# One pass over x about a pivot, single-tile adaLN units and extra adaLN buffers at the start of a layer step

## The chip, the core and the metric

The kernel runs on one core of a Trainium2 chip. The metric is the device time of one execution in microseconds (us). The engines are named as the profile names them: PE is TensorE (PEld its weight load), DVE is VectorE, ACT is ScalarE, POOL is GpSimd, and SP is SyncE, which does no arithmetic here and only issues transfers. "Clock" is the TensorE clock that the chip granted, as a share of full speed.

## The reference, cut to what matters

One layer of a language model, for 256 prompt tokens and 8 samples of 4 tokens, 288 tokens in all, with 2048 features in fp32. What the change touches is the first line of the layer, the modulation and the first normalisation:

```python
mod = silu(c) @ w_ada + b_ada                 # adaLN: 6 x 2048 numbers per sequence (9 sequences)
sh1, sc1, g1, sh2, sc2, g2 = split(mod, 6)
h = layer_norm(x) * (1 + sc1) + sh1           # (x - mean) * rsqrt(var + eps), over the 2048 features
z = h @ w_in                                  # 2048 x 7176
... # two recurrent mixers, w_out, a convolutional feed-forward part (w_up, w_down), two more norms
```

## The kernel before

All activations lie with features on the 128 partitions and tokens along the free axis, so x is 16 tiles (KT) of 128x288. Every weight product is exact to fp32 by halves: a weight block and its input are each split into a high part (`whi`, cast on ACT) and a low part (`wlo`, raw minus high on DVE), and three matmuls are made of each 128x128 block. Weights come in granules of 512 KB (8 blocks, 24 matmuls), one DMA each; `granule()` keeps the raw loads five granules ahead (`load_to`), the high halves three (`high_to`) and the low halves two (`low_to`). The adaLN matrix `w_ada` comes in 512 KB pieces too; an `ada_step` multiplies one of them. Steps are grouped into units: a unit gives the shift and the scale of a few feature tiles of h, and `ADA_K` lists how many tiles the first units give. All of these loads are on SP's queue, in program order, and an issue that finds eight transfers under way waits until the oldest has landed.

`start()` is the stage around the change. It loads c (`ct`), the 16 tiles of x with a DMA each, seven pieces of `w_ada`, then the constants `cs` and `pks` (the bias of adaLN is in the latter). It takes the mean with column sums on PE (`colsum`, `total`: a copy on ACT and a second matmul), subtracts it from each tile (every third tile on POOL, the others on DVE), squares (every fourth on DVE, the others on ACT), sums again, and makes the reciprocal deviation `rx` of it (`rstd_of`). Eight adaLN steps are spread between. Then the product with `w_in` begins in four groups of input tiles (KG = 2, 2, 4, 4): each group runs over 28 output tiles, needs only as many tiles of h as its number says, and adds its partial sums into `z` (`partial`: a copy out of PSUM on ACT for the first group, an addition on DVE for the others). Between the granules come batches of four adaLN steps. When a unit is complete, `ada_finish` transposes it on DVE (`adsb`), adds the bias (`mod`), and queues `hidden(k)` for its tiles: x times `rx`, times the scale, plus the shift, for the prompt and for the samples, and one tick later the split into halves. PSUM has two banks for `mm`, five for `sd`, one for `ad`; a matmul that starts a new sum waits until the bank was read out. DVE, ACT and PE each run in program order.

The lines that the prediction follows, besides the functions below, are these of `low_to` and `high_to`, and the end of the stage in `mixer()`, which loads the rest of `pks` and needs it for a few small DVE operations (`hgrn_lb`) ahead of the next low half:

```python
self.nc.scalar.copy(hi[:, :w], raw[:, :w])                                   # high_to, ACT
self.tt(lo[:, :w], raw[:, :w], hi[:, :w].bitcast(F32), ALU.subtract)         # low_to, DVE
nc.sync.dma_start(self.cs[:, a:], i["cst"][:, a:])                           # mixer
nc.sync.dma_start(self.pks[:, b:], i["pk"][:, b:])
```

Of the kernel before, what the change touches and what calls it, by code (L numbers as in the profile page):

```python
# [10 lines left out]
F32 = mybir.dt.float32  # L11
# [3 lines left out]
ALU = mybir.AluOpType  # L15
PSUM = bass.MemoryType.PSUM

P = 128
D = 2048
KT = 16  # L20
# [3 lines left out]
T = TP + NB * TS  # L24
# [5 lines left out]
EPS = 1e-5  # L30
# [6 lines left out]
NR = 7  # L37
NQ = 5
NA = 7
BATCH = 4  # L40
NS = 4
RATE = 1.3
RA = 2
NPRE = 12
AD0 = 176
# [2 lines left out]
WIDTH = 3  # L48
SPACING = 5
KG = (2, 2, 4, 4, 4)  # L50
ADA_K = (2, 2, 2, 2, 4, 4)
NSPLIT = 28
NUP = 3
LEVELS = (1, 2, 4, 8, 16, 32, 64)
# [71 lines left out]
def _ada_units():  # L126

    u, k = [], 0
    for n in ADA_K:
        u.append([16 * m + k + q for m in range(2) for q in range(n)])  # L130
# [8 lines left out]
class K:  # L139
# [28 lines left out]
    def mm(self, out, lhsT, rhs, start, stop, **kw):  # L168
        self.nc.tensor.matmul(out, lhsT, rhs, start=start, stop=stop, **kw)  # L169
# [112 lines left out]
    def later(self, *fs):  # L282

        def run():
            for f in fs:
                f()
                yield
        self.bg.append(run())
# [7 lines left out]
    def ada_load(self, n):  # L296
        while len(self.ad_raw) < min(n, self.ad_limit):
            s = len(self.ad_raw)
            ahead = 0 <= s - AD0 < NPRE
            if not ahead and s >= (self.ad_n if s < AD0 else max(self.ad_n, AD0 + NPRE)) + NA:  # L300
                break
            if ahead:
                raw = self.pre.tile([P, 1024], F32, tag="apre", name=self.nm("apre"), bufs=NPRE)
            else:
                raw = self.wp.tile([P, 1024], F32, tag="araw", name=self.nm("araw"), bufs=NA)
            self.nc.sync.dma_start(raw, self.i["w_ada"][s])
            self.ad_raw.append(raw)

    def ada_batch(self):

        while self.credit >= BATCH:
            self.credit -= BATCH
            for _ in range(BATCH):
                self.ada_step()

    def ada_step(self):


        s = self.ad_n
        if s >= self.ad_stop:  # L320
            return
        self.ad_n += 1
        self.ada_load(s + NA)
        raw, (u, g) = self.ad_raw[s], STEPS_ADA[s]
        w = 32 * len(UNITS_ADA[u])
        nk = 256 // w
        if g == 0:
            if self.ad_pend is not None and self.ad_pend[0]:
                next(self.ad_pend[1])
            self.ad_ps = self.ps(w, self.ad_tag if u % 2 else "ad")  # L330
        for z in range(nk):
            k = nk * g + z
            for q in range(4):
                c = (4 * z + q) * w
                self.mm(self.ad_ps[32 * q:32 * q + 32], self.csp[:, k, :], raw[:, c:c + w], k == 0, k == KT - 1)
        if k == KT - 1:
            self.ad_pend = [True, None]
            self.ad_pend[1] = self.ada_finish(u, self.ad_ps, self.ad_pend)
            self.bg.append(self.ad_pend[1])
# [69 lines left out]
    def run(self):  # L409
        nc, tc, ctx, i = self.nc, self.tc, self.ctx, self.i  # L410
        self.misc = ctx.enter_context(tc.tile_pool(name="misc", bufs=1))
        self.wp = ctx.enter_context(tc.tile_pool(name="wp", bufs=1))
        self.psum = ctx.enter_context(tc.tile_pool(name="psum", bufs=1, space=PSUM))
        one = self.misc.tile
        self.cs = one([P, NCC], F32, name="cs")
        self.pks = one([P, NPK], F32, name="pks")
        self.mod = one([P, 96, 9], F32, name="mod")
        self.csp = one([P, KT, 32], F32, name="csp")
        self.lm = one([P, len(LEVELS), T // 2], U8, name="lm")
        self.ones = one([P, P], F32, name="ones")  # L420
        nc.gpsimd.memset(self.ones, 1.0)
        self.onesr = one([P, P], F32R, name="onesr")
        nc.gpsimd.tensor_copy(self.onesr, self.ones)
        self.eps = one([P, 1], F32, name="eps")
        nc.gpsimd.memset(self.eps, EPS)
        nc.scalar.preload_act_table_set("natural_log_exp_and_others")
        self.queue_weights()
        self.active, self.bg, self.since, self.credit, self.rate = [], [], 99, 0.0, 0.0
        self.ad_raw, self.ad_n, self.ad_pend, self.h = [], 0, None, []
        self.ad_stop, self.ad_limit, self.ad_tag = AD0 - 4, AD0, "sd"  # L430
        self.start()
        self.mixer()
        self.tail()

    def start(self):

        nc, i = self.nc, self.i
        ct = self.t288()[:, :KT * 9].rearrange("p (k c) -> p k c", c=9)
        nc.sync.dma_start(ct, i["ct"])
        xs = self.xs = [self.t288() for _ in range(KT)]  # L440
        for k in range(KT):
            nc.sync.dma_start(xs[k], i["xt"][:, k, :])
        self.ada_load(NA)
        a, b = CC["cap"][0], PK["b_ada"][1]
        nc.sync.dma_start(self.cs[:, :a], i["cst"][:, :a])
        nc.sync.dma_start(self.pks[:, :b], i["pk"][:, :b])
        nc.gpsimd.memset(self.csp, 0.0)
        e = self.t288()[:, :KT * 9].rearrange("p (k c) -> p k c", c=9)
        self.act(e, ct, AF.Abs)
        self.act(e, e, AF.Exp, scale=-1.0)  # L450
        self.act(e, e, AF.Ln, bias=1.0)
        self.stt(e, ct, 0.0, e, ALU.min, ALU.subtract)
        self.act(e, e, AF.Exp)
        self.tt(self.csp[:, :, 0:9], ct, e, ALU.mult)
        sm = self.ps(T)
        for k in range(KT):
            self.colsum(sm, xs[k], k, KT)
        mu = self.t288()
        self.tsc(mu, self.total(sm), 1.0 / (32 * D), None, ALU.mult)
        self.ada_step()  # L460
        self.ada_step()
        sq = self.ps(T)
        for k in range(KT):
            self.tt(xs[k], xs[k], mu, ALU.subtract, eng=nc.gpsimd if k % 3 == 2 else None)
            s = self.t288()
            if k % 4 == 3:
                self.tt(s, xs[k], xs[k], ALU.mult)
            else:
                self.act(s, xs[k], AF.Square)
            self.colsum(sq, s, k, KT)  # L470
            if k % 4 == 1:
                self.ada_step()
        var = self.t288()
        self.tsc(var, self.total(sq), 1.0 / (32 * D), EPS, ALU.mult, ALU.add)
        self.rx = self.rstd_of(var)
        self.h = []
        self.z = [self.t288() for _ in range(NSPLIT)]
        self.load_to(2)
        for _ in range(2):
            self.tick()  # L480
            self.ada_step()
        k0, done = 0, 0
        for g, ks in enumerate(KG[:-1]):
            while len(self.h) < k0 + ks:
                self.tick()
            nj = GK // ks
            for p in range(NSPLIT // nj):
                hl = self.granule()
                for j in range(nj):
                    ps = self.ps(T, "sd" if j % 2 else "mm")  # L490
                    self.products(ps, hl, j * ks * P, self.h[k0:k0 + ks], True, True)
                    self.tick()
                    self.bg.append(self.partial(self.z[nj * p + j], ps, g == 0))
                self.credit += 2 if done < 14 or done % 3 == 0 else 1
                self.ada_batch()
                done += 1
            k0 += ks
        while len(self.h) < KT:
            self.tick()
# [8 lines left out]
    def hidden(self, k):  # L508
        x = self.xs[k]
        hf = self.t288()  # L510
        self.tt(x, x, self.rx, ALU.mult)
        self.tsc(hf[:, :TP], x[:, :TP], self.mp(1, k), self.mp(0, k), ALU.mult, ALU.add)
        self.tt(self.smp(hf), self.smp(x), self.ms(1, k), ALU.mult)
        self.tt(self.smp(hf), self.smp(hf), self.ms(0, k), ALU.add)
        yield
        self.h.append(self.split(hf))
# [848 lines left out]
    def tail(self):  # L1365
        nc, i, r = self.nc, self.i, self.r
        with self.tc.tile_pool(name="pre", bufs=1) as self.pre:
# [4 lines left out]
            for p in range(KT // 2):  # L1372
# [6 lines left out]
                while self.ad_n < min(AD0, AD0 - 4 + 2 * p):  # L1379
                    self.ada_step()  # L1380
                self.ada_load(AD0 + min(NPRE + NA, 2 * p))
            self.low_to(self.w_used + NL - 1)
# [230 lines left out]
```

## Time and profile before

| | us |
|---|---|
| median of 3 runs | 1605.6 (1604.3 to 1609.29) |
| the profiled execution | 1606.86 |
| its span in the trace | 1605.1 |
| mean granted clock of TensorE in it | 0.985 |
| busy: PE, DVE, ACT, POOL | 1545.0 (96%), 1032.5 (64%), 696.1 (43%), 297.4 (19%) |

The profile is of one execution. A row of its timeline gives the start, the duration or extent of a run of equal instructions, the engine, the line of the code, the operation with its output and inputs, the count, and in brackets how long the engine stood idle before and what released it.

### The profile page before, as it was taken

The numbers are of one execution on the slowest core, as the hardware profiler recorded it, in microseconds if no ns is written. First come the engines' busy times: TensorE is split into PE (matmuls) and PEld (weight loads), VectorE is DVE, ScalarE is ACT, GpSimd is POOL, SyncE is SP. The second block draws the span as 40 slices with busy tenths as digits, with TensorE's granted clock in tenths as the row PEclk, the third lists the DMA queues.
The fourth block names the chain that finished last, engine by engine and source line by source line (L and its number), as shares of the span: only waits on it lengthen the run. The fifth ranks groups of instructions, "written<-read, shape, count | busy, mean of one in ns | idle before, by whom it ended". The sixth has DMA issues, their size and how long they took to land.

```text
span 1605.1 us, 31742 instructions
## 1 busy us (share of the span) xinstructions
PE 1545.0 (96%) x12577; PEld 1449.7 (90%) x12577; DVE 1032.5 (64%) x2068; ACT 696.1 (43%) x1222; POOL 297.4 (19%) x450
## 2 busy tenths in 40 slices
PE   6999989999999989998999999999999999999995
PEld 3999879788898878886999999999999999999994
DVE  4566656888788779778855555455555555555465
ACT  3522325565656555335643433344343333434343
POOL 1000001444353443225311100011110001111012
PEclk9999999999999999998999999999999999999997
DMA  9898855778868778781545455554555555555551
GB/s 337 331 339 325 302 175 159 263 255 302 301 232 294 287 256 312 264 327 64 193 158 170 161 161 171 166 168 162 170 161 159 167 170 170 162 168 158 152 161 60
DMA packets 99268, 340.79 MB, mean 212 GB/s; under 512 B 11432, under 2 KB 18096, under 8 KB 98096
## 3 DMA queue, kind: packets, MB, share of 16 engines
q1 hardware_dynamic: 96624, 328.55, 59.9%
q0 software_dynamic: 2496, 10.22, 1.6%
q8 instruction: 99, 1.62, 0.4%
q14 instruction: 49, 0.40, 0.1%
HBM read 326.51 MB, written 12.21 MB: 211 GB/s over the span
## 4 chain that ended last, share of the span: by engine, by line
PE 83%; DVE 10%; ACT 3%; DMA 3%; issue 1%; SPq 1%; POOL 0%; ACTq 0%; DVEq 0%
PE mm L169 68%; PE sd L169 11%; DVE t L156 4%; PE ad L169 3%; DVE wlo L156 1%; DVE t L159 1%; ACT t L166 1%; DVE t L163 1%; ACT whi L229 1%; DVE c L159 1%; DMA raw<-w_in_b 1%; DMA t<-xt 1%; DMA pks<-pk 1%; DMA raw<-w_out_b 0%; DMA araw<-w_ada 0%
## 5 line engine op out<-in xcount | busy, mean ns | idle before, releaser
L169 PE MATMUL mm<-t,whi 128*128 128x288 f32 (+1 forms) x4624 | 939.2, 298 | 17.0 <-ACT whi L229 9.2
L169 PEld LDWEIGHTS mm<-t,whi 128*128 128x128 f32 (+1 forms) x4624 | 742.9, 189 | 31.3 <-ACT whi L229 12.2
L169 PE MATMUL mm<-t,wlo 128*128 128x288 f32 x2312 | 684.4, 296 | 7.9 <-DVE wlo L156 7.8
L229 ACT CAST whi<-raw 128x1024 fp32r<-128x1024 f32 (+2 forms) x413 | 423.2, 1027 | 472.8 <-PE mm L169 240.2
L156 DVE TENSOR_TENSOR wlo<-raw,whi 128x1024 fp32r<-128x1024 f32 (+2 forms) x413 | 502.7, 1218 | 21.4 <-ACT whi L229 15.9
L169 PEld LDWEIGHTS mm<-t,wlo 128*128 128x128 f32 x2312 | 435.7, 188 | 9.8 <-DVE wlo L156 9.8
L169 PE MATMUL mm<-ff,whi 128*128 128x288 f32 x1376 | 276.1, 296 | 0.0
L169 PEld LDWEIGHTS mm<-ff,whi 128*128 128x128 f32 x1376 | 220.6, 188 | 3.4 <-issue 2.3
L169 PE MATMUL mm<-ff,wlo 128*128 128x288 f32 x688 | 203.1, 295 | 0.0
L166 ACT ACTIVATE t<-t 128x288 f32<-128x288 f32 (+4 forms) x328 | 125.5, 396 | 172.7 <-DVE t L156 111.8
L156 POOL TENSOR_TENSOR t<-t,t 128x288 f32<-128x288 f32 (+3 forms) x159 | 143.1, 909 | 283.9 <-ACT t L166 102.0
L159 DVE SCALAR_TENSOR_TENSOR t<-mm,mod,t 128x256 f32<-128x256 f32 x96 | 46.3, 482 | 149.7 <-PE mm L169 141.6
L169 PEld LDWEIGHTS mm<-ff,wlo 128*128 128x128 f32 x688 | 129.1, 188 | 0.0
L1412 POOL COPY convo<-ext 128x2 f32<-128x2 f32 x43 | 8.0, 186 | 630.4 <-ACT ext L1406 630.4
L156 DVE TENSOR_TENSOR t<-t,t 128x288 f32<-128x288 f32 (+5 forms) x219 | 106.3, 505 | 27.1 <-ACT t L189 20.2
L1407 DVE COPY ext<-mm 128x32 f32<-128x32 f32 x42 | 8.1, 193 | 140.9 <-ACT ext L1406 140.9
L169 PE MATMUL sd<-t,whi 128*128 128x288 f32 x464 | 95.6, 298 | 0.0
L169 PE MATMUL ad<-araw,csp 128*32 128x256 f32 (+1 forms) x1312 | 75.8, 362 | 0.7 <-DMA araw<-w_ada 0.7
L169 PEld LDWEIGHTS sd<-t,whi 128*128 128x128 f32 x464 | 75.8, 192 | 0.0
L156 DVE TENSOR_TENSOR t<-cv,mm 128x256 f32<-128x256 f32 x80 | 20.7, 300 | 79.0 <-PE mm L169 79.0
L169 PE MATMUL sd<-t,wlo 128*128 128x288 f32 x232 | 69.2, 298 | 0.0
L156 DVE TENSOR_TENSOR t<-t,mm 128x288 f32<-128x288 f32 x70 | 31.5, 450 | 56.1 <-PE mm L169 55.8
(233 smaller groups left out, 1151.9 us busy)
## 6 DMA issues: line engine op xcount, KB each, us to landing
araw<-w_ada SPq DMA_DIRECT2D x180, 512.0 KB, 5.4
raw<-w_up_b SPq DMA_DIRECT2D x160, 512.0 KB, 3.6
raw<-w_in_a SPq DMA_DIRECT2D x56, 512.0 KB, 6.8
raw<-w_in_b SPq DMA_DIRECT2D x56, 512.0 KB, 6.5
raw<-w_down SPq DMA_DIRECT2D x48, 512.0 KB, 3.5
raw<-w_down SPq DMA_DIRECT2D x32, 384.0 KB, 3.1
raw<-w_out_a SPq DMA_DIRECT2D x16, 512.0 KB, 6.4
raw<-w_out_b SPq DMA_DIRECT2D x16, 512.0 KB, 5.4
```

Source lines behind the costliest of these rows:

```text
L156: (eng or self.nc.vector).tensor_tensor(out=out, in0=a, in1=b, op=op)
L159: self.nc.vector.scalar_tensor_tensor(out=out, in0=a, scalar=s, in1=b, op0=op0, op1=op1)
L163: (eng or self.nc.vector).tensor_scalar(out=out, in0=a, scalar1=s1, scalar2=s2, op0=op0, **kw)
L166: self.nc.scalar.activation(out, a, f, **kw)
L169: self.nc.tensor.matmul(out, lhsT, rhs, start=start, stop=stop, **kw)
L229: self.nc.scalar.copy(hi[:, :w], raw[:, :w])
L1407: nc.vector.tensor_copy(se[:, :, 2:6], self.smp(pa))
L1412: nc.gpsimd.tensor_copy(co[:, j, 0:2], ext[:, TP:TP + 2])
```

## The change

x is loaded into one tile in a pool that lives only as long as `start()`, by four DMAs of four feature tiles each. The constants and the first three raw granules are issued among the first loads. The mean of the first four feature tiles (the pivot, `piv`) is subtracted from all tiles on DVE; sums of the differences and of their squares (all on ACT) give the mean of the differences `d` and the variance in one pass. `d` is still to be subtracted: for the first two tiles that is done at once, for the other 14 in `hidden()`. Nothing of the first norm is left on POOL. The first two adaLN units have one feature tile each instead of a first unit of two, so there is one unit more in the stage. The odd pieces of `w_ada` below number 64 get five buffers of their own, and loads run up to 12 steps ahead instead of 7. The last of the eight first adaLN steps and the ticks are in another order, with one high half made among them.

```diff
+NE = 5
+EARLY = 64
-ADA_K = (2, 2, 2, 2, 4, 4)
+ADA_K = (1, 1, 2, 2, 2, 4, 4)
...
-            if not ahead and s >= (self.ad_n if s < AD0 else max(self.ad_n, AD0 + NPRE)) + NA:
+            first = s < EARLY and s % 2
+            if s < AD0:
+                mine = sum(1 for z in range(self.ad_n, s) if (z < EARLY and z % 2) == first)
+                if mine >= (NE if first else NA):
+                    break
+            elif not ahead and s >= max(self.ad_n, AD0 + NPRE) + NA:
                 break
-            if ahead:
+            if first:
+                raw = self.early.tile([P, 1024], F32, tag="aearly", name=self.nm("aearly"), bufs=NE)
+            elif ahead:
...
-        self.ada_load(s + NA)
+        self.ada_load(s + NA + NE)
...
-        xs = self.xs = [self.t288() for _ in range(KT)]
-        for k in range(KT):
-            nc.sync.dma_start(xs[k], i["xt"][:, k, :])
-        self.ada_load(NA)
+        xt = xin.tile([P, KT, T], F32, name="x")
+        for k in range(0, KT, 4):
+            nc.sync.dma_start(xt[:, k:k + 4, :], i["xt"][:, k:k + 4, :])
+        xs = self.xs = [xt[:, k, :] for k in range(KT)]
         a, b = CC["cap"][0], PK["b_ada"][1]
+        self.ada_load(8)
+        nc.sync.dma_start(self.pks[:, :b], i["pk"][:, :b])
+        self.load_to(3)
         nc.sync.dma_start(self.cs[:, :a], i["cst"][:, :a])
-        nc.sync.dma_start(self.pks[:, :b], i["pk"][:, :b])
...
-        sm = self.ps(T)
-        for k in range(KT):
-            self.colsum(sm, xs[k], k, KT)
-        mu = self.t288()
-        self.tsc(mu, self.total(sm), 1.0 / (32 * D), None, ALU.mult)
-        self.ada_step()
-        self.ada_step()
-        sq = self.ps(T)
-        for k in range(KT):
-            self.tt(xs[k], xs[k], mu, ALU.subtract, eng=nc.gpsimd if k % 3 == 2 else None)
-            s = self.t288()
-            if k % 4 == 3:
-                self.tt(s, xs[k], xs[k], ALU.mult)
-            else:
+        pv = self.ps(T)
+        for k in range(4):
+            self.colsum(pv, xs[k], k, 4)
+        piv = self.t288()
+        nc.scalar.mul(piv, self.total(pv), 1.0 / (32 * 4 * P))
+        s1, s2 = self.ps(T), self.ps(T)
+        for c in range(0, KT, 4):
+            sq = []
+            for k in range(c, c + 4):
+                self.tt(xs[k], xs[k], piv, ALU.subtract)
+                s = self.t288()
                 self.act(s, xs[k], AF.Square)
-            self.colsum(sq, s, k, KT)
-            if k % 4 == 1:
+                sq.append(s)
+            for k in range(c, c + 4):
+                self.colsum(s1, xs[k], k, KT)
+            for k in range(c, c + 4):
+                self.colsum(s2, sq[k - c], k, KT)
+            if c >= 8:
                 self.ada_step()
         var = self.t288()
-        self.tsc(var, self.total(sq), 1.0 / (32 * D), EPS, ALU.mult, ALU.add)
+        d = self.d = self.t288()
+        self.tsc(d, self.total(s1), 1.0 / (32 * D), None, ALU.mult)
+        self.tt(var, d, d, ALU.mult)
+        self.tsc(var, var, -EPS, None, ALU.add)
+        t2 = self.total(s2)
+        self.stt(var, t2, 1.0 / (32 * D), var, ALU.mult, ALU.subtract)
         self.rx = self.rstd_of(var)
+        for k in range(2):
+            self.tt(xs[k], xs[k], d, ALU.subtract)
...
-        self.load_to(2)
-        for _ in range(2):
+        for n in range(6):
+            self.ada_step()
             self.tick()
-            self.ada_step()
+            if n == 3:
+                self.tick()
+                self.high_to(1)
...
     def hidden(self, k):
         x = self.xs[k]
         hf = self.t288()
+        if k >= 2:
+            self.tt(x, x, self.d, ALU.subtract)
         self.tt(x, x, self.rx, ALU.mult)
```

Three places show how the order of instructions moves. The first is SP's queue at the start. Before, from the end of the first adaLN loads (`araw`) to the third raw granule (`raw_378`):

```order
L445 DMA cs<-cst 128x168
L446 DMA pks<-pk 128x96
L306 DMA araw_168<-w_ada 128x1024
...
L220 DMA raw_324<-w_in_a 128x1024
L220 DMA raw_326<-w_in_a 128x1024
L306 DMA araw_328<-w_ada 128x1024
L306 DMA araw_338<-w_ada 128x1024
L220 DMA raw_378<-w_in_a 128x1024
```

After, from the loads of x on; `aearly` are the pieces of `w_ada` in the new buffers, and `raw_452` is the fourth raw granule:

```order
L453 DMA x<-xt 128x1152 x4
L315 DMA araw_88<-w_ada 128x1024
...
L457 DMA pks<-pk 128x96
L222 DMA raw_105<-w_in_a 128x1024
L222 DMA raw_107<-w_in_a 128x1024
L222 DMA raw_109<-w_in_a 128x1024
L459 DMA cs<-cst 128x168
L315 DMA araw_193<-w_ada 128x1024
...
L315 DMA aearly_411<-w_ada 128x1024
L315 DMA araw_413<-w_ada 128x1024
L222 DMA raw_452<-w_in_a 128x1024
```

Three granules now stand behind 8 adaLN pieces instead of two behind 12 and a third behind 14, and the fourth stands behind 19 where it stood behind 14.

The second place is ACT at the first granules, with what each instruction waits for: a whole-granule cast waits for its DMA, a copy of a partial sum out of PSUM waits for PE. Before:

```order
L229 CAST whi_370<-raw_324 128x1024 [waits DMAHW7_49]
L229 CAST whi_374<-raw_326 128x1024 [waits DMAHW0_49]
L229 CAST whi_380<-raw_378 128x1024 [waits DMAHW3_49]
L503 COPY t_296<-mm_386 128x288 [waits PE_49]
L503 COPY t_297<-sd_393 128x288 [waits PE_49]
L503 COPY t_298<-mm_401 128x288 [waits PE_49]
L229 CAST whi_419<-raw_382 128x1024 [waits DMAHW4_49]
L503 COPY t_299<-sd_409 128x288 [waits PE_49]
L503 COPY t_300<-mm_423 128x288 [waits PE_49]
```

After:

```order
L231 CAST whi_450<-raw_109 128x1024 [waits DMAHW0_49]
L526 COPY t_279<-mm_456 128x288 [waits PE_49]
L526 COPY t_280<-sd_463 128x288 [waits PE_49]
L526 COPY t_281<-mm_471 128x288 [waits PE_49]
L231 CAST whi_489<-raw_452 128x1024 [waits DMAHW5_49]
L526 COPY t_282<-sd_479 128x288 [waits PE_49]
L526 COPY t_283<-mm_493 128x288 [waits PE_49]
L526 COPY t_284<-sd_501 128x288 [waits PE_49]
L526 COPY t_285<-mm_509 128x288 [waits PE_49]
```

The order is the same; the granule whose cast stands between the copies is again the fourth, which is now `raw_452`.

The third place is DVE where a unit of two tiles is complete in the second group. Before (`t_84`, `t_85` are tiles of x, `t_289` is `rx`, `t_300` a partial sum):

```order
L345 STREAM_TRANSPOSE adsb_881<-ad_712 128x128
L159 SCALAR_TENSOR_TENSOR mod<-adsb_881,pks 128x18 x2
L156 TENSOR_TENSOR t_84<-t_84,t_289 128x288
L163 TENSOR_SCALAR t_892<-t_84,mod 128x256
L156 TENSOR_TENSOR t_892<-t_84,mod 128x32
L156 TENSOR_TENSOR t_892<-t_892,mod 128x32
L156 TENSOR_TENSOR t_85<-t_85,t_289 128x288
L163 TENSOR_SCALAR t_897<-t_85,mod 128x256
L156 TENSOR_TENSOR t_897<-t_85,mod 128x32
L156 TENSOR_TENSOR t_897<-t_897,mod 128x32
L156 TENSOR_TENSOR t_300<-t_300,mm_873 128x288
```

After (`x` is the one tile of x, `t_257` is `d`, `t_270` is `rx`, `t_299` a partial sum; the next unit of two is shown):

```order
L354 STREAM_TRANSPOSE adsb_1210<-ad_1039 128x128
L161 SCALAR_TENSOR_TENSOR mod<-adsb_1210,pks 128x18 x2
L158 TENSOR_TENSOR x<-x,t_257 128x288
L158 TENSOR_TENSOR x<-x,t_270 128x288
L165 TENSOR_SCALAR t_1221<-x,mod 128x256
L158 TENSOR_TENSOR t_1221<-x,mod 128x32
L158 TENSOR_TENSOR t_1221<-t_1221,mod 128x32
L158 TENSOR_TENSOR x<-x,t_257 128x288
...
L158 TENSOR_TENSOR t_1227<-t_1227,mod 128x32
L158 TENSOR_TENSOR t_299<-t_299,mm_1202 128x288
```

One operation more stands ahead of each tile's product with `rx`, and so ahead of the addition that reads out the `mm` bank.

## Rows read from the trace of the kernel before

**Rows 1.** Waits of PE from 36 to 205 us: in total, times, longest.

```profile
PE mm L169 <- DVE wlo L156: 0.2, 1, 0.2
```

**Rows 2.** The timeline from 12 to 25 us, the first norm.

```profile
12.75 0.67 PE L169 MATMUL sd<-t,ones 128*32 128x288 f32 x2 [0.21 <-DMA t<-xt]
...
15.19 2.40 DVE L156 TENSOR_TENSOR t<-t,t 128x288 f32<-128x288 f32 x3
15.24 4.94 POOL L156 TENSOR_TENSOR t<-t,t 128x288 f32<-128x288 f32 x5 [13.45 <-DVE t L163]
...
22.38 1.19 DVE L156 TENSOR_TENSOR t<-t,t 128x288 f32<-128x288 f32 x3
...
23.60 0.46 DVE L156 TENSOR_TENSOR t<-t 128x288 f32<-128x288 f32 x1
```

**Rows 3.** The timeline from 29 to 45 us, the first granules.

```profile
29.78 0.45 DVE L156 TENSOR_TENSOR t<-t,t 128x288 f32<-128x288 f32 x1
30.27 0.41 DVE L163 TENSOR_SCALAR t<-t,mod 128x256 f32<-128x256 f32 x1
...
34.87 0.61 PE L169 MATMUL mm<-t,wlo 128*128 128x288 f32 x1 [0.41 <-DVE wlo L156]
...
35.92 1.05 ACT L229 CAST whi<-raw 128x1024 fp32r<-128x1024 f32 x1 [1.41 <-DMA raw<-w_in_a]
...
39.88 0.40 ACT L503 COPY t<-sd 128x288 f32<-128x288 f32 x1
...
42.49 1.95 PE L169 MATMUL sd<-araw,csp 128*32 128x128 f32 x64
...
44.38 0.53 PE L169 MATMUL mm<-t,whi 128*128 128x288 f32 x2
```

**Rows 4.** Stretches: busy time by engine, clock, DMA share, GB/s.

```profile
2.00:15.00 13.00, 9.95 (x41) 2.94 (x45) 0.91 (x3) 1.71 (x6) 0.00 (x0) 1.00 0.93 275
15.00:36.00 21.00, 12.34 (x169) 7.37 (x163) 16.58 (x35) 8.85 (x20) 5.44 (x7) 0.88 1.03 408
15.00:20.00 5.00, 3.68 (x56) 1.77 (x49) 4.93 (x7) 1.66 (x5) 4.76 (x5) 1.00 1.02 419
```

**Rows 5.** The timeline from 69 to 91 us, after two units of two tiles.

```profile
72.65 0.45 DVE L156 TENSOR_TENSOR t<-t,mm 128x288 f32<-128x288 f32 x1
...
73.25 0.51 PE L169 MATMUL mm<-t,whi 128*128 128x288 f32 x2
...
89.85 0.45 DVE L156 TENSOR_TENSOR t<-t,mm 128x288 f32<-128x288 f32 x1
...
90.45 0.51 PE L169 MATMUL mm<-t,whi 128*128 128x288 f32 x2
```

**Rows 6.** The timeline at the ends of the two units of four tiles.

```profile
136.30 1.22 DVE L156 TENSOR_TENSOR wlo<-raw,whi 128x1024 fp32r<-128x1024 f32 x1
...
137.57 0.40 PE L169 MATMUL mm<-t,wlo 128*128 128x288 f32 x1
...
184.27 0.40 PE L169 MATMUL mm<-t,wlo 128*128 128x288 f32 x1 [0.19 <-DVE wlo L156]
```

**Rows 7.** The timeline at the end of the stage.

```profile
203.58 0.46 SPq L531 DMA_DIRECT2D pks<-pk  x1
...
215.26 0.54 PE L169 MATMUL mm<-t,wlo 128*128 128x288 f32 x1 [4.46 <-DVE wlo L156]
```

**Rows 8.** The timeline where PE starts again after other idle spells.

```profile
595.74 0.50 PE L169 MATMUL mm<-t,whi 128*128 128x288 f32 x2 [2.97 <-DVE gt L156]
...
658.08 0.38 PE L169 MATMUL sd<-kd,ones 128*128 128x1 f32 x2 [2.19 <-DVE kd L1224]
```

**Rows 9.** Stretches behind these two spells, columns as in rows 4.

```profile
595.70:600.00 4.30, 4.26 (x44) 3.78 (x48) 2.95 (x8) 3.08 (x9) 2.55 (x3) 1.00 0.19 79
659.00:662.70 3.70, 3.70 (x19) 3.70 (x18) 3.31 (x27) 0.00 (x0) 0.00 (x0) 0.54 0.21 83
```

More of the change, by code (lines that the diff above doesn't have):

```diff
@@ L430, in run, with start @@
         self.ad_stop, self.ad_limit, self.ad_tag = AD0 - 4, AD0, "sd"
-        self.start()
+        with tc.tile_pool(name="early", bufs=1) as self.early:
+            self.start(self.early)
         self.mixer()
         self.tail()
-    def start(self):
+    def start(self, xin):
         nc, i = self.nc, self.i
```

## The prediction

> **What bounds the kernel now.** PE is busy 96% of the span, so I looked first for the places where it is not, and for what it waits on elsewhere in the stretch that the change touches. From 36 to 205 us the view of PE's waits names one wait of 0.2 us [rows 1]: in this stretch whatever is put on PE's path counts in full, and nothing is left there to be won. What can be won lies ahead of it. PE's first complete work on `w_in`, the first product with a low half, stands at 34.87 [rows 3], after the chain of the first norm: the last tile of x at 12.75, the pass of subtractions from 15.19 until 24.06 (23.60 + 0.46) [rows 2], the deviation, h of two tiles, the two halves of the first granule. The second chain to read is that of transfers. From 15 to 36 us they run at 408 GB/s with a DMA share of 1.03, so they are full; from 2 to 15 us, with the tiles of x as 16 loads, they make 275 [rows 4]. The cast of the third granule waited 1.41 us for its transfer and starts with its landing, 35.92 [rows 3]. The reader should see that the stage's start has two limits of nearly the same size, the norm's chain and the queue.
>
> **The first norm.** The transfers moved by the third granule's landing are 13 us at 275 GB/s and 20.9 at 408, 12.1 MB; what stands in the queue up to it (ct 0.07, x 2.36, 14 adaLN pieces 7.34, constants 0.14, three granules 1.57) is 11.5. So a landing comes when some 0.6 MB more than its queue has moved. I use that for the change, with 408 GB/s from about 2.2 us on, since the four loads of x have packets four times as long. The first four tiles (0.07 + 0.59 + 0.6 MB) land at 2.2 + 3.1 = 5.3; the mean took 2.44 from the last landing (12.75 to 15.19) and now has three more column sums behind one landing, at most 0.67 each (one by itself, at 12.75 [rows 2]) and less in a row, I take 0.45: pivot at 9.1. The last four tiles land at 9.7, before their turn. Sixteen subtractions on DVE at 0.40 (1.19 for three without POOL beside them; 0.80 each beside POOL's five) [rows 2] end at 15.5 to 15.7. From the end of the last subtraction to the first product with a low half before, 10.81 us passed (24.06 to 34.87). To this come a second copy of a sum on ACT (0.40), two subtractions of `d` (0.9) and the transpose and bias of a second unit (0.5): 15.6 + 10.8 + 1.8 = 28.2; I say 28.5, since the cast of the first granule now stands between those of the two tiles. The chain gains 6.4 us.
>
> **The queue takes back half of it.** The fourth granule stands behind ct, x, 19 adaLN pieces, constants and three granules: 14.6 MB with itself. With the 0.6 above and 408 GB/s it lands at 2.2 + 15.2/0.408 = 39.5. ACT runs in order: the cast of this granule stands before the copies that empty the `mm` bank, which PE needs for the first block of the third granule (44.38 before, behind the adaLN batch of 42.49 [rows 3]). So that block starts at 39.5 + 1.05 (cast) + 2 x 0.40 (two copies) [rows 3] + 0.1 = 41.5, where the gain of the chain would put it at 38.0. PE idles some 3.5 us there, and the net is 41.5 - 44.4 = **-2.9**. Bounds: at the best stretch's 419 GB/s and nothing moved beyond the queue it lands at 37.1, net -5.3; at a rate as far below 408 as 419 is above it (397) it lands at 40.5, net -1.9. The five new buffers let adaLN pieces go ahead; PE never waited for one from 36 to 205 us [rows 1], so I give them nothing but this cost.
>
> **A rule weighed here.** The trace gives 408 GB/s over 21 us [rows 4]. The Trainium skill, DMA: Bandwidth & Descriptors, section "Where 436 GB/s comes from", says that the fabric could carry 435 GB/s but that transfers between HBM and SBUF are bound by some 358 GB/s per core; by 358 the fourth granule would land at 44.7 and the net would be +2.3 instead of -2.9. The trace disagrees with that bound for a core that runs alone.
>
> **The subtractions of d.** 14 tiles get one more DVE operation in `hidden()`, and the product with `rx` waits for it: 0.49 from one start to the next dependent one (29.78 to 30.27) [rows 3]. They stand in bursts, behind the transpose of a unit that is complete only then, so DVE can't do them earlier. Units of two in the second and third group: PE resumes at 73.25 and 90.45, 0.15 after the addition that empties its `mm` bank, which stands behind the burst [rows 5]; each is later by 2 x 0.49. Units of four: PE resumes at 137.57 and 184.27, 0.05 after the low half that stands behind them (136.30 + 1.22) [rows 6]; each is later by 4 x 0.49. Nothing else covers these four, 5.9 in all. For the unit of two in the first group, where the sums are emptied by ACT, the trace shows no wait, so there is cover of unknown size: from 0 to 1.0, and I take 0.4. Sum **+6.3** (5.9 to 6.9).
>
> **Smaller parts.** With the deeper look-ahead each batch's loads stand one adaLN step later (four steps are 1.95 [rows 3]), and the second part of `pks` behind them; it is issued at 203.58, and small DVE work on it holds a low half until 215.26, PE idle for 4.46 [rows 7]. One step, **+0.5** (0 to 1.3, the time of a 512 KB piece at 408 GB/s). More column sums, the second sum's total and the four squares that go from DVE to ACT lie in a stretch where PE idles; they are in the chain above. A seventh unit holds an `sd` bank after the stage, and nine loads of late adaLN pieces go ahead of weights that have landed for long: 0, at most 1 each.
>
> **The clock.** New idle spells of PE: 3.5 us ahead of 41.5, and about 2.2 in each unit of four (the 1.96 plus what is there). After 2.19 us at 658.08 the clock of 3.7 us was 0.54, that is the lower level of 1.2 GHz; after 2.97 at 595.74 it stayed at 1.00 [rows 8, 9]. So a fall is a matter of its place as well; a stretch of 3.7 us at half speed costs 1.8. Of three spells I take one fall, **+1.8** (0 to 5.4).
>
> **Sum.** -2.9 + 6.3 + 0.5 + 1.8 = +5.7. Against the profiled execution's 1606.9 that is 1612.6; this execution is 1.3 above the median of the runs, so against the median 1605.6 it is 1611.3. I say 1611. About 0.3% (4.8 us) is what a measurement of this kernel can tell from no change, so the bounds are 1600.8 and 1610.4, and the forecast is slower by just over that.
>
> **Rivals.** (1) Not slower: the clock holds through all three spells. For it: 2.97 us without a fall [rows 8, 9]. Then 1609.5, inside the bound; it decides if no spell up to 3.5 us brings the clock down. (2) More falls: two or three, 1613 to 1615. For it: 2.19 was enough at 658.08. (3) The fourth granule lands before 37.5, so that the norm's chain decides alone: net -5.3 to -6.4 instead of -2.9, and one spell less: 1606 to 1607 without a fall, 1608 to 1609 with one. For it: 419 GB/s in one stretch; against it 408 over the whole. The 435 of the page named above would give a landing at 37.1. (4) Faster: the bursts find cover, because PE has other work in the ticks or DVE's operations on the one tile overlap; then at most a third of the 6.3 is paid and no clock falls: -2.9 + 2.1 + 0.5 = -0.3, 1605, and down to 1600 where nothing of it is paid and the granule is early too; below that only if half of the 4.46 at the stage's end goes as well, 1598. Against it: the order of DVE is the same as before but for the added rows, and PE's 0.05 to 0.15 us behind them leave no cover.
>
> **Chances.** Forecast 0.33 (0.25 of it past 1610.4, the rest within), rival 1 0.20 (same), rival 2 0.18 (slower), rival 3 0.13 (same), rival 4 0.16 (0.11 faster, for its low end and for gains that I don't see, 0.05 same). Slower 0.43, same 0.46, faster 0.11. Range: 1602 leaves out a little over the 0.11 below, and 1616 takes in three falls and the upper bounds of the small parts with less than 0.07 beyond.
>
> **What would show it.** In the changed kernel's profile: pivot subtractions from about 9 us, all about 0.40; the first product with a low half near 28.5; the cast of the fourth granule waiting on ACT for its DMA until about 39.5, and PE idle for over 3 us before 41.5; PE waits of about 1.1, 1.1, 2.2 and 2.2 us behind the four bursts, which before sum to 0.2 in the view of waits; POOL idle until the stage's end. The prediction is wrong if the fourth granule's cast doesn't wait, if PE's new waits from 40 to 205 us sum to well under 5 us, if the clock falls more or less often, or if the wait at the end of the stage (4.46) changes by more than a microsecond.

## The result, and the profile after

The changed kernel takes 1617.2 us (median of 5 runs, 1614.35 to 1620.52), the kernel before 1604.3 (5 runs, 1602.37 to 1609.29): a ratio of 1.0082, with an interval from 1.0064 to 1.0099. It is slower, as forecast, but by 12.9 us where 5.7 were worked out, and lies above the range of 1602 to 1616. The profiled execution, 1614.35 with a span of 1612.5, is the fastest of the five, 2.8 us below their median, and the profiled execution of the kernel before (1606.86) lies 2.6 above its own. So the two profiles show only 7.4 us of the difference, and the rest has to come from runs.

The timeline of the start, in the changed kernel: the subtractions of the pivot, PE's first product with a low half, the cast of the fourth granule and PE's third granule.

```profile
8.93 5.99 DVE L158 TENSOR_TENSOR x<-x,t 128x288 f32<-128x288 f32 x16 [4.14 <-ACT t L472]
...
28.93 0.61 PE L171 MATMUL mm<-t,wlo 128*128 128x288 f32 x1 [2.69 <-DVE wlo L158]
...
40.70 1.04 ACT L231 CAST whi<-raw 128x1024 fp32r<-128x1024 f32 x1 [7.12 <-DMA raw<-w_in_a]
...
42.39 0.53 PE L171 MATMUL mm<-t,whi 128*128 128x288 f32 x2 [3.00 <-ACT t L526]
```

The pivot is ready where it was expected (9.1), the chain ends at 28.9 instead of 34.87 [rows 3], and two thirds of that are given back: ACT stands 7.12 us before the fourth granule, the copies that empty the bank stand behind, and PE stands 3.00 us behind them. The third granule begins 2.0 us earlier than before (44.38 [rows 3]).

PE's waits from 36 to 205 us, where before one wait of 0.2 us stood [rows 1]:

```profile
PE mm L171 <- ACT t L191: 3.8, 3, 1.4
PE mm L171 <- ACT t L526: 3.0, 1, 3.0
PE mm L171 <- DVE t L158: 1.2, 2, 1.0
PE mm L171 <- DVE wlo L158: 1.1, 2, 0.5
```

The second line is the start, the others are the bursts, 6.1 us together. The first line is put down to a cast on ACT (L191), but the cast ends beside the addition that empties the bank. At the end of the last unit of four the two pieces of one burst's wait can be read, DVE's addition and PE behind it:

```profile
187.38 0.45 DVE L158 TENSOR_TENSOR t<-t,mm 128x288 f32<-128x288 f32 x1
...
187.98 0.50 PE L171 MATMUL mm<-t,whi 128*128 128x288 f32 x2 [1.35 <-ACT t L191]
...
189.02 0.40 PE L171 MATMUL mm<-t,wlo 128*128 128x288 f32 x1 [0.54 <-DVE wlo L158]
```

PE's product with a low half stands at 189.02; before it stood at 184.27 [rows 6]. From 2.0 us ahead at the third granule to 4.75 behind here is 6.75 us, for 14 subtractions.

The end of the stage: the rest of `pks` is issued, and PE starts again.

```profile
207.49 0.44 SPq L556 DMA_DIRECT2D pks<-pk  x1
...
218.35 0.61 PE L171 MATMUL mm<-t,wlo 128*128 128x288 f32 x1 [2.73 <-DVE wlo L158]
```

The wait of 4.46 [rows 7] is now 2.73, so here 1.7 us come back, and at 218.35 the kernel is 3.1 us late. The surprise lies behind. SP's queue from 388 us on, in the changed kernel, and set among its lines PE at the adaLN batch and where it uses the recurrent state `s`:

```profile
387.64 1.93 PE L171 MATMUL ad<-araw,csp 128*32 128x256 f32 x32
388.34 2.00 SPq L315 DMA_DIRECT2D araw<-w_ada  x4
390.43 0.38 SPq L1029 DMA_DIRECT2D s<-s  x1
390.87 7.42 SPq L222 DMA_DIRECT2D raw<-w_in_b  x3
...
401.87 0.90 PE L171 MATMUL sd<-s,qm 128*32 128x128 f32 x16 [3.94 <-DMA s<-s]
...
408.99 1.76 SPq L315 DMA_DIRECT2D araw<-w_ada  x4
```

The same batches in the kernel before:

```profile
379.25 7.11 SPq L306 DMA_DIRECT2D araw<-w_ada  x4
384.39 1.93 PE L169 MATMUL ad<-araw,csp 128*32 128x256 f32 x32
386.46 0.38 SPq L1004 DMA_DIRECT2D s<-s  x1
386.93 8.95 SPq L220 DMA_DIRECT2D raw<-w_in_b  x3
395.61 0.85 PE L169 MATMUL sd<-s,qm 128*32 128x128 f32 x16 [0.92 <-DVE wlo L156]
395.98 6.50 SPq L306 DMA_DIRECT2D araw<-w_ada  x4
```

Before, the four adaLN loads of a batch are spread over 7 us, because the first of them waits for no step of its batch. There are seven buffers for these pieces: in step s the kernel before loads into the buffer that step s-1 has read, the changed kernel, one piece further ahead, into the one that step s itself reads. So SP now stands before the first load of the batch until PE comes to it (387.64), and then issues all four within 2 us. The state behind them is issued 2.8 us after PE's batch began, where it was 2.1, and lands 11.3 us after its issue, where it took 9.0; PE waits 3.94 us at the product that reads it, where it stood 0.92. The stretches of the changed kernel there, columns as in rows 4:

```profile
388.00:402.00 14.00, 10.05 (x96) 8.62 (x89) 11.96 (x34) 8.29 (x21) 5.57 (x9) 1.00 0.83 317
402.00:409.00 7.00, 7.00 (x63) 6.33 (x63) 5.24 (x10) 5.59 (x14) 2.63 (x4) 0.76 0.30 121
```

While SP stands, the transfers fall to 121 GB/s, and the clock falls to 0.76 after PE's wait. The kernel before has a thin stretch as well (130 GB/s from 368 to 373 us), so the loss of rate is smaller than these rows alone suggest: from 320 to 420 us it is 271 GB/s instead of 279.

### The profile page after: what moved, and what is told of

Read it like the earlier page. It is cut to its first block, busy times and chain, and to the rows that moved or that the text cites. A ratio compares the mean times of both kernels' runs of the same rounds, so it can differ in the third digit from the quotient of the medians.

```text
span 1612.5 us, 32003 instructions
## 1 busy us (share of the span) xinstructions
PE 1540.9 (96%) x12715; PEld 1451.6 (90%) x12715; DVE 1037.3 (64%) x2090; ACT 697.7 (43%) x1228; POOL 290.0 (18%) x445
## 4 chain that ended last, share of the span: by engine, by line
PE 72%; DVE 5%; DMA 2%; ACT 1%; issue 1%; SPq 0%; POOL 0%; ACTq 0%; DVEq 0%
PE mm L171 62%; PE sd L171 6%; PE ad L171 3%; DVE t L158 2%; DVE t L161 1%; DVE wlo L158 1%; DMA s<-s 1%; DMA raw<-w_out_b 1%; DMA t<-xt 0%; ACT whi L231 0%; DMA raw<-w_out_a 0%; ACT t L168 0%; DVE t L165 0%; PE sd L728 0%; DVE tiny L161 0%
## 5 line engine op out<-in xcount | busy, mean ns | idle before, releaser
L168 ACT ACTIVATE t<-t 128x288 f32<-128x288 f32 (+4 forms) x316 | 120.7, 395 | 163.7 <-DVE t L158 101.4
L158 POOL TENSOR_TENSOR t<-t,t 128x288 f32<-128x288 f32 (+3 forms) x154 | 137.6, 902 | 274.1 <-ACT t L168 103.2
L158 DVE TENSOR_TENSOR t<-t,t 128x288 fp32r<-128x288 f32 (+4 forms) x192 | 92.9, 504 | 31.4 <-ACT t L191 25.0
L171 PE MATMUL ad<-araw,csp 128*32 128x256 f32 (+2 forms) x1056 | 61.7, 360 | 0.0
```

The lines of the kernel that those rows point to most:

```text
L158: (eng or self.nc.vector).tensor_tensor(out=out, in0=a, in1=b, op=op)
L168: self.nc.scalar.activation(out, a, f, **kw)
```

## The experiments

All times are medians, and each run had the kernel before beside it (1604.4 to 1604.9).

**The loads from step 64 on as before.**

```diff
-        self.ada_load(s + NA + NE)
+        self.ada_load(s + NA + (NE if s < EARLY else 0))
```

> The changed kernel, but from adaLN step 64 on each step loads as far ahead as in the kernel before (the five buffers and the first 64 steps stay). Theory A (queue): in the changed kernel all four adaLN loads of a batch wait on SP for steps of that same batch, are issued together, and the load of a recurrent state behind them lands late; PE idled 3.94 us for it near 400 us, and the clock fell behind. Then this kernel has no such wait, PE's waits behind 314 us are those of the kernel before, and the time is 3 to 7 us below the changed kernel: 1610 to 1614. Theory B (chance of places): the wait comes from the whole stage being 3 us later against the state's load, or the lost time is the clock alone; then this kernel stays within 2 us of the changed kernel's 1617 and has a wait of 2 us or more on a load in the mixer still.

1608.3 (1605.65 to 1611.8, 10 runs), 1.0024 of the kernel before (1.0011 to 1.0038): 8.9 us below the changed kernel, more than the 3 to 7 of theory A. The batch is spread again. Theory A had no wait on the state any more, but a smaller one is left:

```profile
382.40 7.36 SPq L315 DMA_DIRECT2D araw<-w_ada  x4
389.86 0.37 SPq L1029 DMA_DIRECT2D s<-s  x1
...
399.80 0.85 PE L171 MATMUL sd<-s,qm 128*32 128x128 f32 x16 [1.98 <-DMA s<-s]
```

At 314 us this kernel is as late as the changed kernel (a unit is complete at 314.33 and 314.44, before at 311.21), and from there to the end its profile is 7.1 us shorter. So the lateness of the stage is not the cause, the queue is; theory B is out.

**No extra buffers.**

```diff
-NE = 5
-EARLY = 64
+NE = 0
+EARLY = 0
```

> The changed kernel without the five buffers: adaLN loads as far ahead as before all along, so 14 pieces instead of 19 stand ahead of the fourth granule. Theory A: as with the late loads alone, and besides the fourth granule lands near 34.3 instead of 40.70 (five pieces of 512 KB at 408 GB/s less), so that the wait of 3.0 us on ACT's copy goes and the third granule's first block starts near 39.4 instead of 42.39; 6 to 10 us below the changed kernel, 1607 to 1611. What is left above the kernel before is then the subtractions (about 5). Theory B: only the 3 us at the start are won, 1614.

1606.1 (1603.42 to 1612.56), 1.0015 (0.9997 to 1.0033): 11.1 us below the changed kernel. What is left above the kernel before is 1.7 us, where about 5 were expected. ACT no longer waits for the fourth granule, but the third granule begins only at 41.86, not at 39.4. Without the buffers only seven adaLN pieces go ahead of the granules, the eighth step and with it the second tile's unit come later, and PE's first product with a low half moves from 28.93 to 30.93. I had not counted that.

**The subtractions in the first group.** The operation is taken out of `hidden()`, and two tiles are done at each of the seven granules of the first group.

```diff
                 hl = self.granule()
+                if g == 0:
+                    for k in range(2 * p + 2, 2 * p + 4):
+                        self.tt(self.xs[k], self.xs[k], self.d, ALU.subtract)
...
-        if k >= 2:
-            self.tt(x, x, self.d, ALU.subtract)
```

> The changed kernel with the 14 subtractions of d moved out of hidden() into the seven granules of the first group, two each, where DVE idled 10.6 us from 31.2 to 41.8. Theory A (the subtractions stand on PE's path in the bursts): the waits of PE behind the four bursts, about 1.0, 1.1, 1.9 and 1.9 us, fall to those of the kernel before, and 4.5 to 6 us are won: 1611 to 1613. Rival: PE's wait behind the bursts is a matter of banks and casts (the waits are put down to ACT casts), and the subtractions cost DVE the same elsewhere: within 2 us of 1617.

1612.1 (1608.59 to 1613.73, 6 runs), 1.0039 (1.002 to 1.0057): 5.0 us below the changed kernel, as theory A said. PE's waits from 36 to 205 us in this kernel:

```profile
PE mm L171 <- ACT t L529: 4.0, 1, 4.0
PE mm L171 <- DVE wlo L158: 0.2, 1, 0.2
```

All waits behind bursts are gone, those put down to the casts too. The start is dearer here: 4.0 instead of 3.0 us, and a clock of 0.79 from 42 to 50 us where the changed kernel has 1.00, so that the first unit after the start is complete at 52.78 instead of 50.96. From there to the last unit (177.44 against 180.13) 4.5 us are won. The dearer start need not come from the subtractions. Two later runs, the state on another queue and the state first, have the changed kernel's program up to 280 us; their waits there are 3.5 and 3.6 us, their first unit is complete at 52.45 and 52.68, and the clock is 0.79 in both. The stretch in this run, columns as in rows 4:

```profile
42.00:50.00 8.00, 7.32 (x43) 7.32 (x44) 5.65 (x9) 5.57 (x14) 0.00 (x0) 0.79 0.90 356
```

The same stretch in the run with the state first:

```profile
42.00:50.00 8.00, 7.42 (x44) 7.42 (x45) 3.64 (x3) 5.56 (x14) 0.00 (x0) 0.79 0.92 363
```

From that unit to the last one the two later runs take 130.2 us, this run 124.7, so against them 5.5 us are won, a fall of the clock behind a burst in each of them included.

**The buffers alone, on the kernel before.** `NE`, `EARLY`, the new part of `ada_load` and the pool are put into the kernel before; norm, units and order of the first loads stay.

```diff
+NE = 5
+EARLY = 64
...
-        self.ada_load(s + NA)
+        self.ada_load(s + NA + NE)
```

> The kernel before with the five buffers and the deeper look-ahead alone. Theory A: the loads of each batch come together from step 64 on and a state's load lands late: 2 to 6 us slower than the kernel before, 1606 to 1610, with a PE wait on a load of a state in the mixer. Theory B (the loss is from the later stage, not from the queue): within 2 us of the kernel before.

1613.7 (1608.22 to 1618.86, 10 runs), 1.0051 (1.0032 to 1.0069): 9.3 us slower. More than either theory gave, since there the extra pieces go ahead of the first granule too, and PE begins late (33.61 before):

```profile
39.16 0.85 PE L171 MATMUL mm<-t,whi 128*128 128x288 f32 x2 [11.90 <-ACT whi L231]
```

Its stage is 6.6 us late at the first unit behind the start (59.57 against 52.96), and 8.6 at 319.82. The profile, of the slowest of the ten executions, loses 3.4 us more behind that. It names no wait on a state, which theory A had asked for; but PE stands 2.77 us ahead of the product with `s` at 406.09, and the state, issued at 395.57, lands 10.4 us later, at 406.0.

**Both repairs.** The two edits of the second and the third run together.

> The changed kernel without the five buffers and with the subtractions of d moved into the first group's granules: both repairs together. Theory A (two separate costs, the queue's 11 us by the runs so far and the bursts' 5): they add, 1617.2 - 11 - 5 = 1601, some 3 us faster than the kernel before, which is what is left of the 6 us by which the norm's chain is shorter. PE starts its third granule near 39.4 and no PE wait over 0.5 us stands between 40 and 205 us. Rival (the two share one cause, the later stage against the transfers): 1604 to 1606, no better than without the buffers alone.

1597.6 (1596.7 to 1602.04), 0.9959 of the kernel before (0.9944 to 0.9974): 7.3 us faster than before. Each repair by itself gives 11.1 and 5.0, both in one kernel 19.5; the 3.4 beyond the sum lie within what the intervals leave open, so the costs add, as theory A said. Its third granule begins behind an adaLN batch of 38.94 and 1.96, at 40.8, later than the 39.4 expected, for the reason seen without the buffers. That is 3.6 us ahead of the kernel before, and near 307 us it is 4.2 (306.99 against 311.21); the profile, of the slowest of the six executions, doesn't show where the rest of the 7.3 is won. From 36 to 205 us PE waits as little as before:

```profile
PE mm L171 <- DVE wlo L158: 0.2, 1, 0.2
```

**Units of two tiles.** The same with `ADA_K = (2, 2, 2, 2, 4, 4)`.

> As the kernel with both repairs, but the first adaLN units have two tiles as before. Theory A says that the single-tile units only order the start: the first high half waits for all eight adaLN steps either way, and PE's first product with a low half moves by 1 us or less; within 2 us of the kernel with both repairs. Rival (the seventh unit and the other parity of its banks cost time in the mixer): 2 to 4 us faster than it.

1597.3 (1594.59 to 1601.96), 0.9958 (0.9943 to 0.9972). No difference in time, though PE's first product with a low half comes at 31.43 instead of 30.02: more than the 1 us of theory A, and no cost of the seventh unit.

**The state on another queue.**

```diff
-        nc.sync.dma_start(s0, self.i["s0"][h])
+        nc.gpsimd.dma_start(s0, self.i["s0"][h])
```

> The changed kernel with the load of the recurrent state s issued from POOL's queue instead of SP's; all else stays. Theory A1 (the late state load is the cost of the look-ahead): the PE wait of 3.94 us on it goes and with it the fall of the clock, 4 to 8 us below the changed kernel's 1617. Theory A2 (the weights that stand behind the four loads on SP cost as much as the state): the wait goes, but only 1 to 3 us are won, because waits for low halves and casts of weights appear in its place.

1622.2 (1621.56 to 1622.67, 4 runs), 1.0108 (1.0092 to 1.0124): 5 us slower than the changed kernel, and neither theory had that. In its profile 2.6 us are lost before the first load of `s` at 293.7, where the clock fell twice (the last unit of four is complete at 182.70 instead of 180.13), and the two intervals overlap; so what the edit itself costs is not known to better than some 4 us. The load stands among POOL's own work and is issued at 394.97, 4.5 us later than by SP, and it lands 11.4 us after its issue:

```profile
394.97 0.60 POOL L1029 DMA_DIRECT2D s<-s  x1
...
406.45 0.86 PE L171 MATMUL sd<-s,qm 128*32 128x128 f32 x9 [6.07 <-DMA s<-s]
```

So SP's queue itself isn't what makes the transfer slow. What is under way when it starts is the likely reason, but no run varies that alone. Whether the state is most of the loss, the run doesn't tell.

**The buffers from step 8 to 63 only, subtractions in the first group.**

```diff
-        self.ada_load(s + NA + NE)
+        self.ada_load(s + NA + (NE if 8 <= s < EARLY else 0))
```

> The changed kernel with the subtractions moved, the five buffers used only from step 8 to 63, and loads from step 64 on as before. Theory A: the buffers are neutral if they neither go ahead of the fourth granule nor change the batches from step 64 on; same time as the kernel with both repairs within 2 us, 1600 to 1603. Rival (deeper look-ahead in the first stage delays the granules behind it also after the start): 2 us or more above it, with ACT waiting for granules and PE for ACT between 45 and 130 us.

1598.0 (1595.66 to 1604.06, 12 runs), 0.9962 (0.9949 to 0.9975): as with both repairs. The fourth granule lands at 34.37 (40.70 in the changed kernel), the first unit behind the start is complete at 47.30. With the pieces ahead of that granule it was 50.96 in the changed kernel, and 52.78 where the subtractions are moved as here but the clock fell; so they cost 3.7 us there, and 5.5 with the fall. Used so, the buffers are neutral.

**The state first.** The two lines that allocate and load `s` are moved up by one slot, ahead of the batch on SP.

> The changed kernel with the load of the recurrent state s issued one slot earlier, still on SP, so that it stands ahead of the batch's four adaLN loads and of a granule instead of behind them. The run with the state on POOL's queue couldn't tell, since POOL issued it 4.5 us later still. Theory A1 (the state that lands behind the batch is most of the cost of the deeper look-ahead): no PE wait on s is left, and the time is 4 to 8 us below the changed kernel's 1617: 1609 to 1613. Theory A2 (the batch delays everything behind it, and the state is only the first to show): the wait goes, but 1 to 3 us are won, 1614 to 1616.

1613.9 (1611.86 to 1617.21, 4 runs), 1.0058 (1.004 to 1.0075): 3.3 us below the changed kernel, between the theories, and the two intervals overlap. The state is now issued at 380.70, and the wait on it is gone:

```profile
380.70 0.37 SPq L1018 DMA_DIRECT2D s<-s  x1
...
400.55 0.85 PE L171 MATMUL sd<-s,qm 128*32 128x128 f32 x16
```

The largest of PE's waits from 316 to 770 us (`gt` and `kd` are tiles of the mixers):

```profile
PE mm L171 <- DVE gt L158: 4.1, 3, 1.6
PE sd L171 <- DVE kd L1249: 3.8, 1, 3.8
```

The first was 5.2 in the changed kernel and 4.1 before. The second has grown: it was 2.5 in the changed kernel, 2.2 before, and 0.8 with the loads from step 64 on as before. All lines of the view sum to 16.9 us, where the changed kernel has 19.3 and the kernel before 15.4. From the unit near 314 us to the end this profile takes 1294.1 us, the changed kernel 1298.1, the kernel before 1293.9, and the one with late loads 1291.0. So in this execution the state's new place gives back 4.0 us, nearly all that the changed kernel's profile lost there against the kernel before (4.2), but not all that late loads give back (7.1); whether the late state is the whole cost stays open. In all, the two profiles lie only 1.2 us apart, because the first stage of this one is 2.7 us later (317.17 against 314.44), with two falls of the clock.

**One step deeper, on the kernel before.**

```diff
-        self.ada_load(s + NA)
+        self.ada_load(s + NA + (1 if s >= 64 else 0))
```

> The kernel before with one thing changed: from adaLN step 64 on each step loads one piece further ahead, so that each load waits for the step in which it is issued. No other buffers, norm or units are touched. Theory A: that alone costs what the changed kernel lost behind its first stage, 6 to 9 us by the difference between the changed kernel and the one with late loads (1617.2 and 1608.3): 1610 to 1614 with a fall in the transfer rate while SP waits for PE. Rival (the one step costs only in company with the five buffers or the shifted stage): within 2 us of the kernel before, 1603 to 1607.

1609.8 (1607.13 to 1612.94, 10 runs), 1.0027 (1.0016 to 1.0038): 5.1 us slower with nothing else touched, a little less than theory A gave. The batch is issued in one piece (1.75 us), the state behind it lands late:

```profile
388.29 1.75 SPq L306 DMA_DIRECT2D araw<-w_ada  x4
390.14 0.44 SPq L1004 DMA_DIRECT2D s<-s  x1
...
401.12 0.89 PE L169 MATMUL sd<-s,qm 128*32 128x128 f32 x16 [3.23 <-DMA s<-s]
```

## Why the prediction was wrong in size

**The norm's chain** was right. 28.5 was worked out for the first product with a low half, 28.93 was measured: 5.9 us gained where 6.4 were counted. With the other costs taken away (both repairs) 7.3 us are won, but that is no second proof of it: there the chain ends at 30.02, and the profile shows 3.6 us at the third granule.

**The fourth granule** was right as a mechanism and a little small: landing at 40.70 instead of 39.5, a net of -2.0 instead of -2.9. The 408 GB/s that the estimate used is what the changed kernel has from 30 to 36 us too, and the start is better fed than before (275 [rows 4]):

```profile
2.00:15.00 13.00, 8.07 (x79) 5.12 (x79) 6.61 (x18) 7.70 (x23) 0.00 (x0) 1.00 1.01 384
30.00:36.00 6.00, 6.00 (x34) 6.00 (x33) 1.15 (x2) 1.20 (x3) 0.00 (x0) 0.67 1.03 408
```

The 384 in place of the 408 that I had assumed from 2.2 us on is 0.2 MB less by 15 us, 0.6 us of the 1.2. Whether it is the longer packets of x that feed the start better, as the prediction had it, no run shows by itself. The 358 GB/s per core of the Trainium skill (DMA: Bandwidth & Descriptors, section "Where 436 GB/s comes from"), which the prediction set aside, do not bind here either: these two stretches lie above it.

**The subtractions** were right: 6.3 predicted, 6.75 between the third granule and the last burst in the profile; moved away they give 5.0 by the medians with the queue's loss in place, 8.5 without it (1606.1 to 1597.6). The second figure holds falls of the clock as well, two behind the bursts in the profile without the buffers (0.50 from 140 to 142 us and from 192 to 194), none in the one with both repairs.

**The clock** came out near the forecast, though the changed kernel's own profile doesn't show it. I counted one fall in the three new spells of the stage. In that profile none of them (3.00, and 1.35 and 0.54 behind a unit of four) brought it down, while the spell of 3.94 behind the state did (0.76 from 402 to 409). But it is the fastest of five executions, and three other profiles have the same program up to the last unit of four. In the one with the state on another queue and the one with the state first the clock fell behind the spell at the start, 3.5 and 3.6 us there (0.79 from 42 to 50), and behind the first unit of four (0.59 and 0.64 from 142 to 144). In the one with late loads it held behind 2.8 us at the start, but fell behind the first unit of four (0.50 from 140 to 142) and, where its loads already differ, behind the second (0.50 from 192 to 194). So spells of one length behind a unit of four bring the clock down in one execution and not in another; the prediction had put that down to the place of a spell.

**The stage as a whole** held. For the time at the unit near 314 us the terms give 3.9 us late without a fall of the clock and 7.5 with two. The changed kernel's profile is 3.2 late without one; the profiles with the state on another queue and with the state first, with two, are 5.8 and 6.0 late (316.96 and 317.17 against 311.21). What the sum lacks lies behind that unit.

**The step that failed** is that of the smaller parts: "With the deeper look-ahead each batch's loads stand one adaLN step later", priced at +0.5 (0 to 1.3) for the end of the stage alone. The event was seen, but only its last load was priced, and only where the stage ends. It recurs with each batch in the mixer. What it does there is not to delay one piece by a step: a load that could be issued at once is turned into one that blocks SP until PE reaches the batch, so that transfers run dry and then four pieces go out together in front of whatever follows. The run with the loads from step 64 on as before puts 8.9 us on it, the run on the kernel before 5.1. At the end of the stage itself it cost nothing: the rest of `pks` is issued 3.8 us after PE's adaLN batch ahead of it began (203.73), where it was 4.7 (198.93), and the wait there became 1.7 us shorter. A change of that wait by more than a microsecond was one of the prediction's own signs of being wrong.

The sum without clock and this term, -2.9 + 6.3, was 3.4; with the loads repaired the kernel is 3.9 above the kernel before. What stays open is why the look-ahead costs 3.8 us more in the changed kernel than alone. In the profiles both lose it in the same places (from 326 to 426 us 99.36 us pass between two loads of a state `c` in the changed kernel, 99.26 with one step alone, 95.49 before, 94.75 with late loads). The intervals of the three runs leave some 4 us of play in that difference, and the clock falls differ from execution to execution, so it may be no more than that; this is argued only.

## What to carry to other kernels

A deeper look-ahead isn't free where loads share an in-order queue: write down which event each issue waits for, since a load that waits for the step that is just running holds up all behind it, then releases them in a heap. Ask of each load that is put ahead what critical load now stands behind it, at the start and in every later stage that runs the same code. And an operation that is put into a burst which ends last for the busy engine costs its full time, while the same 14 operations showed no cost in a stretch where their engine idles. And one profile is one execution: where the same program was traced under other edits, read the stage there too, before a forecast of the clock is called wrong.

## What the runs showed of the hardware beyond that

A 512 KB load of the state that was issued behind a batch of others was there 11.3 us after its issue from SP's queue and 11.4 from POOL's; the same load took 9.0 in the kernel before, 10.7 issued ahead of the batch, and the fastest load of this tensor 3.0. And the executions of one program differ by more than one profile can tell: the changed kernel's five runs reach from 1614.35 to 1620.52 with mean clocks from 0.980 to 0.985, and its first stage was traced with no fall of the clock behind its new spells and, under other edits, with two.
